# Two feed-forwards in five sets: the down products among the next set's tiles

## The chip, the cores and the metric

One core of a Trainium2 chip. The metric is the device time of one launch in microseconds. Engines: PE (TensorE, matrix products), DVE (VectorE), ACT (ScalarE), POOL (GpSimd), SP (SyncE, which issues the loads of weights). Products accumulate in PSUM, everything else lies in SBUF.

## What is computed

512 tokens of width 1024 pass two blocks in float32. The first block has two layers, each a mixer (a pooling mixer in layer 0, latent attention in layer 1) and a feed-forward, every one behind a norm and added to x:

```python
D_FF = ((8 * D_MODEL // 3 + 255) // 256) * 256
...
def swiglu(h, w_gate, w_up, w_down):
    return (jax.nn.silu(h @ w_gate) * (h @ w_up)) @ w_down
```

D_FF is 2816. The second block is a differential attention and a mixture of 16 experts with a hierarchical router. The change lies in the two feed-forwards of the first block, and by one number in the loads ahead of the experts.

## The kernel before

**Products.** x lies transposed, 8 pieces of 128 features by 512 tokens (`x[:, d]`). Every float32 operand is split into a high part rounded to fp32r and a low part, the rest; `mm3` makes three products (high x high, low x high, high x low) into one accumulator. Splitting a weight costs one ACT copy (`hi<-raw`) and one subtraction on DVE or POOL (`lo<-raw,hi`) per 512 columns.

**Stages in the trace.** Pooling mixer 0 to 36 us, feed-forward of layer 0 36 to 390, latent attention to 569, feed-forward of layer 1 569 to 927, differential attention to about 1197, routing to 1240, experts to 1519, and the end.

**One feed-forward.** `ffn` walks 22 tiles of 128 hidden features in sets, `SETS` = (0 to 8), (8 to 15), (15 to 22). A tile has gate and up weights in one load of 1 MB (`ffn_gu`, 128x2048). Its two results give silu(gate) times up, split into `hh`, `hl`. After a set's tiles, eight down products follow, one for each d of 128 output features, over the set's 7 or 8 hidden tiles (`ffn_dn`, 448 or 512 KB each), and each is added into `x[:, d]`. The rule for a tile has three forms:
- `plain(j)` for the first five: 2 x 8 x 3 products of 512 columns on `xh`, `xl`, while `mixed_x` makes sums and differences of the halves of the tokens.
- `later()` for tile 5 and for the tiles 1 and 4 of the later sets (`BETWEEN`): also 48 products of 512 columns, on the even and odd pieces (`bh`, `bl`).
- `mixed()` for the others, 12 per layer: seven products over half the rows and half the tokens each (Strassen's scheme with 7 instead of 8), 84 matmuls of 256 columns, from sums of quarters of the weights. Additions on DVE put the seven accumulators together (`t`, `u`); ACT takes the silu; then `t<-t,u`, `hh`, `hl`.

**The stream of weights.** `Stream` keeps one list of items in order of use. It has 2 raw buffers and 3 each for high and low parts (`BUFS`). `load` issues a DMA on SP as soon as a raw buffer has been handed back; in the queue it waits there for the last operation that read the buffer. `split_mixed` is the split of a mixed tile in eight steps: POOL adds r + s (`rs<-raw`) and subtracts p - r (`raw<-raw`); ACT and DVE split p, q (1024 wide), then rs; DVE makes rs - p (`raw<-rs,raw`) and q minus that (`raw<-raw`); one 512-wide split; and last q, r, s together, 1536 wide, whose `lo` hands the raw buffer back. `split_part` splits other items by 512 columns; the second part of a down load goes to POOL (`POOLED`). The calls `ws.pump()` between products do one step each; `go()` does one step of the list `tail`, which holds the end of a tile (hidden parts). Each engine works strictly in the order in which the code issues its instructions, so the places of `pump` and `go` set the order of DVE. Nearly all instructions are recorded under the helper's line, 447; the loads under 136.

**After the layers.** In the last set `after(d)` makes what the next stage needs of each finished d (`xh`, `xl`, squares summed in `ss`). `AHEAD` says how many pieces of expert weights may be loaded into free buffers before the routing is done.

Of the kernel before, what the change touches and what calls it, by code (L numbers as in the profile page):

```python
# [9 lines left out]
F32R = mybir.dt.float32r  # L10
# [3 lines left out]
OP = mybir.AluOpType  # L14
# [3 lines left out]
P = 128  # L18
# [3 lines left out]
KT = D // P  # L22
FF = 2816
FT = FF // P


SETS = ((0, 8), (8, 15), (15, 22))
PLAIN = 6
BETWEEN = (1, 4)
H = T // 2  # L30


# [7 lines left out]

AHEAD = (24, 28, 32)
PIECES = 5
CHUNKS = 7
LASTS = 2
# [44 lines left out]
class Stream:  # L91
# [473 lines left out]
class Net:  # L565
# [346 lines left out]
    def ffn(self, l, hooks, after, extra=None):  # L912
# [3 lines left out]
        nc = self.nc  # L916
        hooks = list(hooks)
        xh, xl = self.held
        parts = [[] for _ in range(7)]
        full = []  # L920
        mix = self.mixed_x(l, full, parts)
        hh, hl, pend = [], [], []

        tail = []
# [7 lines left out]
        def rest():  # L932
            while tail:
                go()

        def hidden(t):
            hh.append(self.tmp("hh", F32R))
            hl.append(self.tmp("hl", F32R))
            h, r = hh[-1], hl[-1]
            nc.scalar.activation(h, t, AF.Copy)  # L940
            yield
            nc.vector.tensor_tensor(r, t, h.bitcast(F32), op=OP.subtract)

        def evac(pg, pu):
            t, u = self.tmp("t"), self.tmp("u")
            nc.vector.tensor_tensor(t, pg, self.R, op=OP.mult)
            nc.scalar.activation(t, t, AF.Silu)
            nc.vector.tensor_tensor(u, pu, self.R, op=OP.mult)
            yield
            nc.vector.tensor_tensor(t, t, u, op=OP.mult)  # L950
            yield from hidden(t)

        def plain(j):
            wh, wl = self.ws.take()
            pp = []

            def mm(m, k, begin, end):
                o = (2 * m + k % 2) * T + k // 2 * P
                c = slice(o, o + P)
                self.mm3(pp[m], wh[:, c], wl[:, c], xh[k], xl[k], begin, end)  # L960

            if j == PLAIN - 2:
                pp += [self.acc(), self.acc()]
                for k in range(KT):
                    for m in range(2):
                        mm(m, k, k == 0, k == KT - 1)
                    xh[k] = xl[k] = None
                    if k < 2:
                        go()
                    if k > 1:  # L970
                        next(mix, None)
                    if k == 4:
                        self.ws.pump(4)
            else:
                for m in range(2):
                    pp.append(self.acc())
                    for n, k in enumerate((0, 2, 4, 6, 1, 3, 5, 7)):
                        mm(m, k, n == 0, n == KT - 1)
                        if n in (0, 2):
                            go()  # L980
                        if not hooks and n in (1, 3, 6):
                            next(mix, None)
                    self.ws.pump(3)
                    if hooks:
                        hooks.pop(0)()
            self.ws.release()
            pend.append(pp)
            if not hooks:
                while pend:
                    tail.append(evac(*pend.pop(0)))  # L990
                    go()

        def later():
            wh, wl = self.ws.take()
            pp = []
            for m in range(2):
                ps = self.acc()
                for n, k in enumerate((0, 2, 4, 6, 1, 3, 5, 7)):
                    o = (2 * m + k % 2) * T + k // 2 * P
                    c = slice(o, o + P)  # L1000
                    self.mm3(ps, wh[:, c], wl[:, c], *full[k], n == 0, n == KT - 1)
                    go()
                    self.ws.pump()
                pp.append(ps)
            self.ws.release()
            t = self.tmp("t")
            nc.scalar.activation(t, pp[0], AF.Silu)
            nc.vector.tensor_tensor(t, t, pp[1], op=OP.mult)
            tail.append(hidden(t))
            go()  # L1010

        def mixed():
            g, s = self.tmp("t"), self.tmp("u")
# [22 lines left out]
            for n in range(7):  # L1036
                if n % 2 == 0:
                    ps = self.acc()
# [13 lines left out]
                    nc.scalar.activation(g, g, AF.Silu)  # L1052
            add(s0, s0, bank[6])
            nc.vector.tensor_tensor(g, g, s, op=OP.mult)
            tail.append(hidden(g))
            go()

        for f0, f1 in SETS:
            hh.clear()
            hl.clear()  # L1060
            for j in range(f0, f1):
                if j < PLAIN - 1:
                    plain(j)
                elif j < PLAIN:
                    for _ in mix:
                        pass
                    later()
                elif self.plain(j):
                    later()
                else:  # L1070
                    mixed()
            rest()
            for d in range(KT):
                wh, wl = self.ws.take()
                ps = self.acc()
                n = f1 - f0
                for f in range(n):
                    c = slice(f * P, (f + 1) * P)
                    self.mm3(ps, wh[:, c], wl[:, c], hh[f], hl[f], f == 0, f == n - 1)
                    if f % 3 == 1:  # L1080
                        self.ws.pump()
                self.ws.flush()
                self.ws.release()
                nc.vector.tensor_tensor(self.x[:, d], ps, self.x[:, d], op=OP.add)
                if f1 == FT:
                    after(d)

    def plain(self, j):
        return j < PLAIN or any(f0 and j - f0 in BETWEEN for f0, f1 in SETS if f0 <= j < f1)

    def ffn_weights(self, l, arena=0):
        for f0, f1 in SETS:
            for j in range(f0, f1):
                self.ws.add(self.a["ffn_gu"][l, j], j < arena, not self.plain(j))
            for d in range(KT):
                self.ws.add(self.a["ffn_dn"][l, d, :, f0 * P:f1 * P])


    def rope_tables(self):
# [1286 lines left out]
def _host(inp):  # L2386

    f = np.ascontiguousarray
    o = {}
# [6 lines left out]
    def twice(v):  # L2396
# [11 lines left out]
    gu = np.stack([inp["ffn_w_gate"], inp["ffn_w_up"]], axis=0)  # L2408
    o["ffn_gu"] = f(gu.reshape(2, 2, KT // 2, 2, P, FT, P).transpose(1, 5, 4, 0, 3, 2, 6)
                    .reshape(2, FT, P, 2048))  # L2410
    o["ffn_dn"] = f(inp["ffn_w_down"].reshape(2, FT, P, KT, P).transpose(0, 3, 2, 1, 4)
                    .reshape(2, KT, P, FT * P))

    wd = inp["mla_w_down"][0]
    wd = np.concatenate([wd, wd[:, 512:]], axis=1)
# [26 lines left out]
    r = np.arange(P)  # L2442
# [4 lines left out]
    c = np.arange(T)[None, :] - 3 * P - r[:, None]  # L2447
# [58 lines left out]
```

## Time and profile before

| | us |
|---|---|
| median of 3 runs | 1537.18 (1536.66 to 1541.72) |
| the profiled execution | 1539.18 |
| its span in the trace | 1537.4 |
| PE busy | 1487.6 |
| DVE busy | 1088.1 |
| ACT busy | 815.8 |
| POOL busy | 414.0 |

The profile records one execution; the span runs from the first to the last instruction, and 1.8 us of the execution's time lie outside. Mean granted clock of PE: 0.983 of full speed. A duration in the trace is one instruction's own; where instructions overlap in an engine's pipeline, the distance of their starts is what each costs.

### The profile page before, as it was taken

To read this page: it belongs to the slowest core of one execution; us is meant where nothing else is said; L and a number is where in the kernel's file an instruction comes from. 1 tells how busy PE (TensorE), PEld (TensorE's weight loads), DVE (VectorE), ACT (ScalarE), POOL (GpSimd) and SP (SyncE) were. 2 spreads that over 40 slices of the span, in tenths; PEclk is the share of its full clock that TensorE was granted. 3 is DMA by queue.
4 is the path that set the end of the run, shared out by engine and by line. 5 is a ranking of instruction groups with operands and counts; after the bars stand their busy time and mean duration, and the time that the engine had idled before them with its cause. 6 is when DMAs were issued, how large, how long until landed. Compare 5 with 4: busy or idle time off the path is not lost.

```text
span 1537.4 us, 23426 instructions
## 1 busy us (share of the span) xinstructions
PE 1487.6 (97%) x8561; PEld 1250.4 (81%) x8561; DVE 1088.1 (71%) x1948; ACT 815.8 (53%) x1609; POOL 414.0 (27%) x330
## 2 busy tenths in 40 slices
PE   8999999999999999999999999999979799999996
PEld 7788898998878878888989989999968566666664
DVE  6795684775578747945746766888985487878774
ACT  5443343344466534423423454787774377777774
POOL 3322322222341103233222224222312222222321
PEclk9999999999999999999999999999979799999998
DMA  6124223224211112152232242122048799999991
GB/s 218 60 71 122 87 93 115 107 80 127 81 64 49 49 55 93 65 158 104 74 117 105 79 127 84 56 83 95 31 135 305 216 323 347 368 363 356 367 316 26
DMA packets 72247, 221.72 MB, mean 144 GB/s; under 512 B 7872, under 2 KB 17216, under 8 KB 58944
## 3 DMA queue, kind: packets, MB, share of 16 engines
q1 hardware_dynamic: 58752, 201.03, 37.6%
q0 software_dynamic: 4064, 14.16, 4.0%
q10 hardware_dynamic: 9312, 5.01, 1.1%
q8 instruction: 68, 1.11, 0.3%
q14 instruction: 51, 0.42, 0.1%
HBM read 208.63 MB, written 11.53 MB: 143 GB/s over the span
## 4 chain that ended last, share of the span: by engine, by line
PE 82%; DVE 7%; ACT 5%; DMA 2%; issue 1%; POOL 1%; ACTq 0%; POOLq 0%; SPq 0%; DVEq 0%
PE acc L447 70%; PE pss L447 8%; PE pst L447 4%; DVE lo L447 1%; DVE bl L447 1%; ACT hi L447 1%; ACT p L447 1%; DMA raw<-ffn_gu 1%; DVE xl L447 1%; DMA bnd<-bands 1%; DVE t L447 1%; DVE p L447 1%; DVE x L447 0%; DMA out<-ring,idx 0%; DVE xe L447 0%
## 5 line engine op out<-in xcount | busy, mean ns | idle before, releaser
L447 ACT ACTIVATE hi<-raw 128x512 fp32r<-128x512 f32 (+3 forms) x354 | 235.7, 697 | 211.2 <-PE acc L447 95.8
L447 POOL TENSOR_TENSOR lo<-raw,hi 128x512 fp32r<-128x512 f32 (+2 forms) x125 | 167.0, 1340 | 629.7 <-ACT hi L447 600.4
L447 PE MATMUL acc<-bl,hi 128*128 128x256 f32 (+1 forms) x832 | 252.5, 304 | 0.0
L447 PE MATMUL acc<-bh,hi 128*128 128x256 f32 (+1 forms) x832 | 252.5, 303 | 0.0
L447 PE MATMUL acc<-bh,lo 128*128 128x256 f32 (+1 forms) x832 | 252.4, 303 | 0.0
L447 DVE TENSOR_TENSOR lo<-raw,hi 128x512 fp32r<-128x512 f32 (+2 forms) x229 | 230.9, 1010 | 28.5 <-ACT hi L447 28.0
L447 DVE TENSOR_TENSOR wl<-raw,wh 128x512 fp32r<-128x512 f32 x288 | 203.0, 748 | 53.0 <-ACT wh L447 46.0
L447 ACT ACTIVATE wh<-raw 128x512 fp32r<-128x512 f32 x320 | 177.5, 620 | 0.0
L447 PEld LDWEIGHTS acc<-bl,hi 128*128 128x128 f32 x832 | 159.0, 191 | 6.6
L447 PEld LDWEIGHTS acc<-bh,hi 128*128 128x128 f32 x832 | 159.0, 191 | 6.6
L447 PEld LDWEIGHTS acc<-bh,lo 128*128 128x128 f32 x832 | 159.0, 191 | 6.3
L447 DVE TENSOR_TENSOR x<-acc,x 128x512 f32<-128x512 f32 x75 | 51.4, 689 | 128.7 <-PE acc L447 128.6
L447 PE MATMUL acc<-hl,hi 128*128 128x512 f32 x352 | 137.1, 390 | 0.2 <-DVE hl L447 0.2
L447 PE MATMUL acc<-hh,hi 128*128 128x512 f32 x352 | 137.1, 390 | 0.2 <-ACT hh L447 0.2
L447 PE MATMUL acc<-hh,lo 128*128 128x512 f32 x352 | 136.9, 389 | 0.0
L447 PE MATMUL acc<-hi,xh 128*128 128x256 f32 x384 | 111.6, 291 | 0.0
L447 PE MATMUL acc<-lo,xh 128*128 128x256 f32 x384 | 109.2, 284 | 0.6 <-DVE lo L447 0.6
L447 PE MATMUL acc<-hi,xl 128*128 128x256 f32 x384 | 109.0, 284 | 0.0
L447 PE MATMUL acc<-wh,teh 128*96 128x512 f32 x224 | 103.1, 460 | 0.2 <-ACT teh L447 0.2
L447 PE MATMUL acc<-wl,teh 128*96 128x512 f32 x224 | 88.2, 394 | 0.8 <-DVE wl L447 0.8
L447 PE MATMUL acc<-wh,tel 128*96 128x512 f32 x224 | 88.5, 395 | 0.0
L447 PE MATMUL acc<-xh,hi 128*128 128x512 f32 x200 | 79.8, 399 | 1.2 <-ACT xh L447 1.2
(349 smaller groups left out, 3349.9 us busy)
## 6 DMA issues: line engine op xcount, KB each, us to landing
raw<-moe_w SPq DMA_DIRECT2D x200, 256.0 KB, 8.1
raw<-moe_w SPq DMA_DIRECT2D x46, 1024.0 KB, 11.1
raw<-ffn_gu SPq DMA_DIRECT2D x43, 1024.0 KB, 4.8
raw<-ffn_dn SPq DMA_DIRECT2D x32, 448.0 KB, 3.3
raw<-da_in SPq DMA_DIRECT2D x12, 1024.0 KB, 5.0
raw<-ffn_dn SPq DMA_DIRECT2D x16, 512.0 KB, 3.5
raw<-mla_up SPq DMA_DIRECT2D x4, 832.0 KB, 4.4
raw<-mla_o_a SPq DMA_DIRECT2D x12, 256.0 KB, 3.5
```

The lines of the kernel that those rows point to most:

```text
L447: r = f(*args, **kw)
```

## The change

- `SETS` becomes five sets of 4, 4, 4, 5 and 5 tiles; `BETWEEN` goes, so all 16 tiles from the seventh on are mixed (84 matmuls of 256 columns), and only tile 5 is `later`.
- The down products of a set come among the next set's tiles. `ffn_order` gives the order of everything: after a tile, `down` for a pair of d (two accumulators, 2 x 4 or 2 x 5 hidden tiles x 3 products); after tile 5 two pairs, after tiles 6 to 15 and 17 to 20 one, after 16 and 21 none; the last set's eight d follow at the end. Down weights are repacked in pairs of d on the host (`ffn_dn0` to `ffn_dn4`, 512 or 640 KB).
- These accumulators come from the pool `pss`, those of the last set from `acc`. The addition into x goes into `tail`, so `go` issues it, a few products later.
- `hh`, `hl` come from `pair`, so that two sets' hidden parts can live at once.
- `AHEAD` for the second phase is 27 instead of 28.

```diff
-SETS = ((0, 8), (8, 15), (15, 22))
+SETS = ((0, 4), (4, 8), (8, 12), (12, 17), (17, 22))
 PLAIN = 6
-BETWEEN = (1, 4)
...
-AHEAD = (24, 28, 32)
+AHEAD = (24, 27, 32)
...
-            tail.append(hidden(t))
+            tail.append(hidden(t, hh, hl))
...
+        def down(n, i):
+
+            f0, f1 = SETS[n]
+            his, los = sets[n]
+            wh, wl = self.ws.take()
+            last = n == len(SETS) - 1
+            for m in range(2):
+                while len(tail) > 1:
+                    go()
+                ps = self.acc() if last else self.pss()
+                for f in range(f1 - f0):
+                    c = slice((m * (f1 - f0) + f) * P, (m * (f1 - f0) + f + 1) * P)
+                    self.mm3(ps, wh[:, c], wl[:, c], his[f], los[f], f == 0, f == f1 - f0 - 1)
+                    if f % 2:
+                        go()
+                        self.ws.pump()
+                d = 2 * i + m
+                if last:
+                    self.ws.flush()
+                    rest()
+                    nc.vector.tensor_tensor(self.x[:, d], ps, self.x[:, d], op=OP.add)
+                    after(d)
+                else:
+                    tail.append(add(d, ps))
+            self.ws.release()
...
+    def ffn_order(self):
+
+
+        todo = []
+        for n, (f0, f1) in enumerate(SETS):
             for j in range(f0, f1):
...
+                yield "tile", n, j
+                if j >= PLAIN - 1:
+                    for _ in range(-(-len(todo) // (f1 - j))):
+                        yield "down", n - 1, todo.pop(0)
+            todo = list(range(KT // 2))
+        for i in todo:
+            yield "down", len(SETS) - 1, i
...
     def ffn_weights(self, l, arena=0):
...
+        for kind, n, i in self.ffn_order():
+            if kind == "tile":
+                self.ws.add(self.a["ffn_gu"][l, i], i < arena, i >= PLAIN)
+            else:
+                self.ws.add(self.a[f"ffn_dn{n}"][l, i])
```

How this moves instructions shows at two places. The first is the queue of SP, which issues the loads of weights, in layer 0. Before, a set's gate-up loads follow each other, then its eight down loads:

```order
L136 DMA raw<-ffn_gu 128x2048 x8
L136 DMA raw<-ffn_dn 128x1024 x8
L136 DMA raw<-ffn_gu 128x2048 x7
L136 DMA raw<-ffn_dn 128x896 x8
L136 DMA raw<-ffn_gu 128x2048 x7
L136 DMA raw<-ffn_dn 128x896 x8
```

With the change the same queue reads so from its first gate-up load:

```order
L134 DMA raw<-ffn_gu 128x2048 x6
L134 DMA raw<-ffn_dn 128x1024 x2
L134 DMA raw<-ffn_gu 128x2048
L134 DMA raw<-ffn_dn 128x1024
L134 DMA raw<-ffn_gu 128x2048
L134 DMA raw<-ffn_dn 128x1024
L134 DMA raw<-ffn_gu 128x2048
L134 DMA raw<-ffn_dn 128x1024
L134 DMA raw<-ffn_gu 128x2048
```

It goes on in this way; the sets of five stand here:

```order
L134 DMA raw<-ffn_gu 128x2048
L134 DMA raw<-ffn_dn 128x1024
L134 DMA raw<-ffn_gu 128x2048 x2
L134 DMA raw<-ffn_dn 128x1280
L134 DMA raw<-ffn_gu 128x2048
L134 DMA raw<-ffn_dn 128x1280
L134 DMA raw<-ffn_gu 128x2048
```

Gate-up and down loads now alternate from tile 6 on, except between the tiles 16 and 17.

The second place is DVE in layer 0 in the steady part, from the split of one mixed tile's weights to the end of that split. `raw` is the loaded weights, `rs` the sum of two quarters, `t` and `u` the two results of the tile before, `acc` and `pss` accumulators. Before, with two mixed tiles behind each other or a plain one behind a mixed one (here the latter):

```order
L447 TENSOR_TENSOR lo<-raw,hi 128x1024
L447 TENSOR_TENSOR u<-t,acc 128x256
L447 TENSOR_TENSOR t<-t,acc 128x256
L447 TENSOR_TENSOR u<-u,acc 128x256
L447 TENSOR_TENSOR raw<-rs,raw 128x512
L447 TENSOR_TENSOR lo<-rs,hi 128x512
L447 TENSOR_TENSOR u<-u,acc 128x256
L447 TENSOR_TENSOR t<-t,u 128x512
L447 TENSOR_TENSOR hl<-t,hh 128x512
L447 TENSOR_TENSOR raw<-raw 128x512
L447 TENSOR_TENSOR lo<-raw,hi 128x512
L447 TENSOR_TENSOR lo<-raw,hi 128x1536
```

With the change, a mixed tile with a down pair behind it:

```order
L445 TENSOR_TENSOR u<-t,acc 128x256
L445 TENSOR_TENSOR t<-t,acc 128x256
L445 TENSOR_TENSOR u<-u,acc 128x256
L445 TENSOR_TENSOR raw<-raw 128x512
L445 TENSOR_TENSOR u<-u,acc 128x256
L445 TENSOR_TENSOR t<-t,u 128x512
L445 TENSOR_TENSOR hl<-t,hh 128x512
L445 TENSOR_TENSOR lo<-raw,hi 128x512
L445 TENSOR_TENSOR x<-pss,x 128x512
L445 TENSOR_TENSOR lo<-raw,hi 128x1536
L445 TENSOR_TENSOR x<-pss,x 128x512
L445 TENSOR_TENSOR lo<-raw,hi 128x512
```

The rows of the split stand between the previous tile's additions in both; new are two additions into x (`x<-pss,x`), one ahead of the 1536-wide `lo` and one behind it, and the `lo` of the down weights after them.

In all, PE has 8901 matmuls where it had 8613; on the operands of `later` and `mixed` (`bh`, `bl`) 32 of 512 columns remain of 160 for each kind of product, and 896 of 256 columns stand where 672 did. Additions into x number 106 where 75 were (42 from `acc`, 64 from `pss`).

## Rows read from the trace of the kernel before

**Rows 1.** The page: span; busy time of each engine (share of the span, instructions).

```profile
span 1537.4 us, 23426 instructions
...
PE 1487.6 (97%) x8561; PEld 1250.4 (81%) x8561; DVE 1088.1 (71%) x1948; ACT 815.8 (53%) x1609; POOL 414.0 (27%) x330
```

**Rows 2.** Windows: busy us of PE, PEld, DVE, ACT, POOL; PE clock granted, DMA share, GB/s.

```profile
105.00:390.00 285.00, 285.00 (x1733) 256.66 (x1732) 183.93 (x269) 110.04 (x175) 75.00 (x54) 1.00 0.31 100
...
640.00:927.20 287.20, 286.78 (x1739) 257.53 (x1737) 182.60 (x268) 115.14 (x182) 78.23 (x67) 1.00 0.32 104
...
1240.00:1519.00 279.00, 278.53 (x1288) 181.44 (x1289) 223.34 (x359) 210.87 (x417) 73.73 (x56) 1.00 0.94 324
```

**Rows 3.** Timeline of PE in layer 0: start, duration, engine, line, operation, tiles, shape, count.

```profile
168.87 0.28 PE L447 MATMUL acc<-bh,hi 128*128 128x256 f32 x1
...
178.94 0.40 PE L447 MATMUL acc<-bh,hi 128*128 128x512 f32 x1
...
189.85 0.28 PE L447 MATMUL acc<-bh,hi 128*128 128x256 f32 x1
```

**Rows 4.** Timeline of DVE in layer 0, 169 to 187 us.

```profile
169.68 1.75 DVE L447 TENSOR_TENSOR lo<-raw,hi 128x1536 fp32r<-128x1536 f32 x1
...
177.71 0.42 DVE L447 TENSOR_TENSOR u<-t,acc 128x256 f32<-128x256 f32 x1 [0.76 <-PE acc L447]
178.16 0.42 DVE L447 TENSOR_TENSOR t<-t,acc 128x256 f32<-128x256 f32 x1
178.50 0.41 DVE L447 TENSOR_TENSOR u<-u,acc 128x256 f32<-128x256 f32 x1
...
181.28 0.41 DVE L447 TENSOR_TENSOR u<-u,acc 128x256 f32<-128x256 f32 x1
181.79 0.69 DVE L447 TENSOR_TENSOR t<-t,u 128x512 f32<-128x512 f32 x1
183.19 1.00 DVE L447 TENSOR_TENSOR hl<-t,hh 128x512 fp32r<-128x512 f32 x1 [0.70 <-ACT hh L447]
184.11 1.77 DVE L447 TENSOR_TENSOR raw<-rs,raw 128x512 f32<-128x512 f32 x1
185.81 0.68 DVE L447 TENSOR_TENSOR lo<-rs,hi 128x512 fp32r<-128x512 f32 x1
186.41 0.68 DVE L447 TENSOR_TENSOR raw<-raw 128x512 f32<-128x512 f32 x1
```

**Rows 5.** Timeline of SP (DMA issues) and POOL, the same stretch.

```profile
171.46 0.33 SPq L136 DMA_DIRECT2D raw<-ffn_gu  x1
...
177.01 0.33 SPq L136 DMA_DIRECT2D raw<-ffn_gu  x1
...
181.82 1.82 POOL L447 TENSOR_TENSOR rs<-raw 128x512 f32<-128x512 f32 x1 [2.15 <-DMA raw<-ffn_gu]
183.72 1.62 POOL L447 TENSOR_TENSOR raw<-raw 128x512 f32<-128x512 f32 x1
```

**Rows 6.** DMA issues of gate and up weights, median us to landing: all; the slowest alone.

```profile
raw<-ffn_gu SPq DMA_DIRECT2D x39, 1024.0 KB, 4.8
...
raw<-ffn_gu SPq DMA_DIRECT2D x1, 1024.0 KB, 7.2
```

**Rows 7.** Groups of DVE, 640 to 927.2 us: busy, mean ns, idle before and what ended it.

```profile
L447 DVE TENSOR_TENSOR wr<-wr,vecs 128x160 f32<-128x160 f32 x1 | 0.3, 326 | 1.6 <-DMA wr<-router 1.6
```

**Rows 8.** Timeline of DVE, one of the last eight down products of layer 1.

```profile
898.84 0.69 DVE L447 TENSOR_TENSOR x<-acc,x 128x512 f32<-128x512 f32 x1 [0.93 <-PE acc L447]
900.32 0.75 DVE L447 SCALAR_TENSOR_TENSOR xl<-x,gg,xh 128x512 fp32r<-128x512 f32 x1 [0.79 <-ACT xh L447]
...
902.19 0.68 DVE L447 TENSOR_TENSOR lo<-raw,hi 128x512 fp32r<-128x512 f32 x1
```

**Rows 9.** Windows at the start of layer 1: a pause of PE and the stretch after.

```profile
573.90:576.90 3.00, 1.50 (x6) 0.51 (x4) 1.43 (x3) 2.70 (x5) 0.29 (x1) 1.00 0.69 292
576.90:583.70 6.80, 6.80 (x21) 5.74 (x21) 3.97 (x4) 2.18 (x5) 5.39 (x4) 0.50 0.35 114
```

More of the change, by code (lines that the diff above doesn't have):

```diff
@@ L934, in rest, with hidden @@
                 go()
[L936 to L939, printed above, removed]
+        def hidden(t, his, los):
+            h, r = self.pair("h")
+            his.append(h)
+            los.append(r)
             nc.scalar.activation(h, t, AF.Copy)
@@ L942, in hidden, with evac @@
             nc.vector.tensor_tensor(r, t, h.bitcast(F32), op=OP.subtract)
-        def evac(pg, pu):
+        def evac(his, los, pg, pu):
             t, u = self.tmp("t"), self.tmp("u")
@@ L950, in evac @@
             nc.vector.tensor_tensor(t, t, u, op=OP.mult)
-            yield from hidden(t)
+            yield from hidden(t, his, los)
         def plain(j):
@@ L986, in plain @@
             self.ws.release()
-            pend.append(pp)
+            pend.append([hh, hl] + pp)
             if not hooks:
@@ L1054, in mixed @@
             nc.vector.tensor_tensor(g, g, s, op=OP.mult)
-            tail.append(hidden(g))
+            tail.append(hidden(g, hh, hl))
             go()
-        for f0, f1 in SETS:
-            hh.clear()
-            hl.clear()
-            for j in range(f0, f1):
[L1062 to L1086, printed above, removed]
@@ L1088, in plain @@
-    def plain(self, j):
-        return j < PLAIN or any(f0 and j - f0 in BETWEEN for f0, f1 in SETS if f0 <= j < f1)
-    def ffn_weights(self, l, arena=0):
[L1092 to L1096, printed above, removed]
+        def down(n, i):
[22 more added lines that the diff above has]
+            self.ws.release()
@@ new lines, in add @@
+        def add(d, ps):
+            nc.vector.tensor_tensor(self.x[:, d], ps, self.x[:, d], op=OP.add)
+            return
+            yield
+        sets = {}
+        for kind, n, i in self.ffn_order():
+            if kind == "down":
+                if (n, i) == (len(SETS) - 1, 0):
+                    rest()
+                    parts = full = None
+                down(n, i)
+                if i == KT // 2 - 1:
+                    sets.pop(n)
+                continue
+            if i == SETS[n][0]:
+                hh, hl = [], []
+                sets[n] = hh, hl
+            if i < PLAIN - 1:
+                plain(i)
+            elif i < PLAIN:
+                for _ in mix:
+                    pass
+                later()
+            else:
+                mixed()
@@ new lines, in ffn_order @@
+    def ffn_order(self):
+        todo = []
+        for n, (f0, f1) in enumerate(SETS):
+            for j in range(f0, f1):
+                yield "tile", n, j
[5 more added lines that the diff above has]
+            yield "down", len(SETS) - 1, i
+    def ffn_weights(self, l, arena=0):
+        for kind, n, i in self.ffn_order():
+            if kind == "tile":
+                self.ws.add(self.a["ffn_gu"][l, i], i < arena, i >= PLAIN)
+            else:
+                self.ws.add(self.a[f"ffn_dn{n}"][l, i])
@@ L2410, in _host @@
                     .reshape(2, FT, P, 2048))
-    o["ffn_dn"] = f(inp["ffn_w_down"].reshape(2, FT, P, KT, P).transpose(0, 3, 2, 1, 4)
-                    .reshape(2, KT, P, FT * P))
+    dn = inp["ffn_w_down"].reshape(2, FT, P, KT // 2, 2, P).transpose(0, 3, 2, 4, 1, 5)
+    for n, (f0, f1) in enumerate(SETS):
+        o[f"ffn_dn{n}"] = f(dn[:, :, :, :, f0:f1].reshape(2, KT // 2, P, 2 * (f1 - f0) * P))
     wd = inp["mla_w_down"][0]
```

## The prediction

> **What bounds the kernel now.** I read the page first: TensorE (PE) is busy 97% of the span [rows 1]. Then the windows, to see whether that holds where the change lies: from 105 to 390 us, most of feed-forward layer 0, PE has no idle time at all, and from 640 to 927.2 us, layer 1, it misses 0.4 us [rows 2]. So in both feed-forwards the time is the number of PE products times their pitch, as long as the other engines keep ahead. The reader should note VectorE (DVE) in the same rows: 184 of 285 us, 65%, so it has room on the average. What the average does not tell is the order in which DVE works, and that decides here. Next the timeline of PE for the two prices: a mixed tile runs from 168.87 to 178.94, which is 10.07 us for 84 products, 0.120 each; the plain tile behind it from 178.94 to 189.85, 10.91 us for 48 products of 512 columns, 0.227 each [rows 3]. Last, the timelines of DVE, SP and POOL for how a tile's weights get ready.
>
> **Fewer PE cycles.** Four tiles per layer turn from plain to mixed, eight in all: 8 x (10.91 - 10.07) = 6.7 us less. The down products keep their number (22 x 24 per layer, 0.227 each), only their order changes. One pair of them costs 4 x 6 x 0.227 = 5.45 us with 4 tiles in the set and 5 x 6 x 0.227 = 6.81 with 5. In the steady part PE thus needs 10.07 + 5.45 = 15.52 us per cycle (a mixed tile and a pair), later 16.88.
>
> **A loop through one raw buffer.** There are two raw buffers. Before, loads of gate and up weights follow each other, so the one for the tile after next starts when the first buffer comes free, and a tile's split has a whole spare tile of PE time. In the new order of SP's queue gate-up and down loads alternate, so with two buffers every gate-up load lands in the same one: it waits for DVE's last subtraction (128x1536) of the tile just before. That subtraction stands late in DVE's order, behind the previous tile's last additions and the first addition into x. Load, split and next load form a closed loop with one tile in it, and PE is not part of it. Its length:
> - Issue to POOL's first operation: 177.01 to 181.82, 4.81 us; the median landing says 4.8 [rows 5, 6].
> - POOL's two operations, 181.82 to 183.72 + 1.62: 3.52 us [rows 5]. DVE's raw<-rs needs both; I add 0.08 as an estimate.
> - Then DVE back to back. A 512-wide operation takes a slot of 0.60 (185.81 to 186.41); the additions take 0.45 (177.71 to 178.16) and 0.34 (178.16 to 178.50); the last addition takes 0.51 (181.28 to 181.79); the product t<-t,u, with ScalarE's rounding behind it, 1.40 (181.79 to 183.19) [rows 4]. In the new order: raw<-rs 0.60, lo<-rs 0.60, u 0.45, t 0.34, u 0.34, raw<-raw 0.60, u 0.51, t<-t,u 1.40, hl 0.60, lo 0.60, x<-pss 0.60, lo of 1536 1.75 [rows 4]. Sum 8.39.
> - The next issue comes 0.03 behind: 169.68 + 1.75 = 171.43, issue at 171.46 [rows 4, 5].
>
> Together 4.81 + 3.52 + 0.08 + 8.39 + 0.03 = 16.83 us. That is 1.31 more than PE's 15.52 in a cycle with a set of 4, and 0.05 less than 16.88 with 5. The addition x<-pss is new: no row has it. Its nearest row is an operation of the same width, 0.60; it might be hidden in a wait (0) or take 1.17 more when POOL runs beside it, as raw<-rs did (1.77 from 184.11, against a slot of 0.60) [rows 4]; I take 0.60.
>
> **How long the lead lasts.** PE needs the third split part of a tile at its third product, 24 x 0.120 = 2.9 us after the tile's start and that part's lo is followed by x (0.60) and the 1536-wide lo (1.75), so the latter ends about 2.3 us later. So PE stalls where that subtraction ends later than 5.2 us after its tile starts. Tile 6 is got ready beside plain tiles, its subtraction ends about when the tile starts: a lead of 5.2. Every cycle takes 1.31 of it, and in layer 0 operations of the rope tables in DVE's order take about 0.6 more in most of them. By tile 9 the lead is gone (3 x 1.9 = 5.7, a stall of 0.5). Tiles 10 to 16 pay 1.31 each, 9.2, and three rope operations at 0.6 are in the loop with them, 1.8. Layer 0: 11.5 us. Between tiles 16 and 17 there is no down pair, so the load for 17 starts early and the cycles with 5 stay just even. In layer 1 the rope work is gone, but the router's multiply stands in DVE's order within tile 7's cycle and waits for its own load, 1.6 us now [rows 7]; I put its harm at 3 (estimate: that wait and what stands behind it), so tile 8 pays 0.5 and tiles 9 to 16 pay 8 x 1.31 = 10.5: 11.0 us. Both: 22.5 us.
>
> **The ends of the layers.** The last set's eight products are 15 x 0.227 = 3.4 us each, before 4.8. In layer 1 DVE takes 898.84 to 902.19 + 0.68, 4.03 us, per product for x, xl, the two square sums and a split [rows 8]. It falls behind by 0.62 each; the eighth xl comes at about 3.5 + 7 x 4.03 + 2.2 = 33.9 us, while PE wants it after 27.2 + 42 x 0.120 = 32.3. I take 1.9 with the square sum (0.5 if some splits move away, 3 if all stay). In layer 0 the chain has one square sum less and about keeps up: 0.5. Together 2.4.
>
> **The rest.** The first set of layer 1 lost about 1 us to a late down load; that load now comes in another place, I take 0.5 less (0 to 1). One routing piece less ahead: in the expert stage PE misses 0.5 of 279 us while DMA is 94% busy [rows 2], one 0.73 us slot at most; 0. The planner reorders part of the attention stage: 0, between -3 and +3.
>
> **Sum** against the profiled execution (1539.2 us, 1.8 outside its span; 2.0 above the median of the runs): 1539.2 - 6.7 + 22.5 + 2.4 - 0.5 = 1556.9, which is 1555 on the footing of the median.
>
> **Rivals.**
> - *The loop does not close.* If one cycle stays under PE's 15.52, which needs 1.3 us less than I count, there is no stall: -6.7 + 2.4 - 0.5 gives 1532, and 1530 if the ends cost little. For it: DVE has room on the average [rows 2], and 1.40 of my sum is a wait that other work could fill. Against: DVE works in the written order, and I counted slots, no waits of PE. The point of decision is 15.52.
> - *Half a loop.* The load lands quicker, or the lead is longer than 5.2 because the first cycles run free; the stalls are then 5 to 15 us: 1537 to 1548.
> - *The clock falls.* At the start of layer 1 PE paused (1.50 us busy of 3.00), and in the next 6.8 us the granted clock was 0.50, the lower level: 21 products where 30 fit at the full one [rows 9]. If the stall in each tile did the same, PE alone would need more than the loop: (30 - 21) x 0.227 = 2 us per cycle, less the 1.3 that it idles, over some 16 cycles 11 to 30 us: 1566 to 1585. Against: the stalls of 1.3 us are shorter, and PE is busy otherwise. The Trainium skill (TensorE: Matmul & The Clock Gate, section HAM oscillation — how this bites in real kernels) describes just this, a wait in every weight tile after which each tile begins at half clock; no repeated pause of this kind is in the trace of before. By it, the time would be the one just given.
> - *POOL gets ahead.* POOL's split of the down weights is ready some 0.6 us after DVE's 1536-wide subtraction begins. If it starts first, the subtraction is stretched as raw<-rs was, by 1.17 [rows 4], and the loop is 18.0: 16 x 1.2 + 8 x 1.1 more, 1583. The Trainium skill (SBUF — State Buffer, section Who interferes with whom) calls the port between the two an exclusive lock, with whoever issues first blocking the other; the stretched row agrees.
> - *The change does not do what it says.* The new program has 32 of the 512-wide products on each of the plain tile's operand pairs where it had 160, so the tiles are mixed indeed; I give this no chance.
>
> **Numbers.** The loop binds: 0.62, with its own range 1550 to 1566 (a load that lands 0.4 later because a down load is issued some 2 us behind it, where the slowest took 7.2 [rows 6], costs 16 x 0.4 and some for the sets of 5: +9). Half a loop: 0.18. It does not close: 0.14. Clock or POOL: 0.06. A difference of 0.3%, 4.6 us, is about what a measurement of this kernel can tell from none. Faster by more: the third case and a little of the second, 0.15; within: 0.10, out of the second; slower: 0.75. The range goes from 1532, which takes in about half of the third case, to 1566.
>
> **What would show it.** In the changed profile: PE pauses of about 1.3 us in tiles 9 or 10 to 16 of each layer, ended by DVE's lo; gate-up loads issued right behind the 1536-wide lo, about 16.8 us apart; no pauses in the cycles of 5; each feed-forward 7 to 9 us longer than before, stalls and savings together; the wait for xl or ss at the end of layer 1. Wrong would be gate-up loads issued less than 15.5 us apart with PE still full, or pauses ended by something else.

## The result and the profile after

The changed kernel took 1575.11 us (median of 4), the kernel before beside it 1536.92: a ratio of 1.0242, with a 95% interval of 1.0222 to 1.0261. It is slower, as forecast, but by 38 us where 18 had been forecast; the range ended at 1566.

The page of the changed kernel, against [rows 1] (in the third row: a group of products, its busy time and mean, and behind the second bar the idle time of PE ahead of it and what ended most of it):

```profile
span 1574.8 us, 24096 instructions
...
PE 1495.6 (95%) x8849; PEld 1267.6 (80%) x8849; DVE 1136.4 (72%) x2074; ACT 830.4 (53%) x1617; POOL 435.2 (28%) x323
...
L445 PE MATMUL acc<-bh,lo 128*128 128x256 f32 (+1 forms) x928 | 270.9, 292 | 21.9 <-DVE lo L445 21.9
```

The time of products rose by 8 us only, although the change takes matmul time away; 21.9 us of the rest are PE's waits for DVE's lo in the mixed tiles. Where the 38 us lie is read from windows cut at the first product of each stage (feed-forward 0, latent attention, feed-forward 1, the differential attention up to its last output product, the rest; columns as in [rows 2]):

```profile
36.50:402.80 366.30, 354.02 (x2179) 319.28 (x2179) 270.00 (x413) 150.89 (x236) 113.73 (x72) 0.99 0.26 92
402.80:583.30 180.50, 174.81 (x971) 146.67 (x970) 119.74 (x237) 95.48 (x216) 39.12 (x31) 1.00 0.15 49
583.30:955.70 372.40, 358.67 (x2177) 323.02 (x2176) 265.08 (x405) 151.58 (x236) 111.39 (x80) 0.98 0.29 103
955.70:1242.80 287.10, 268.27 (x1924) 251.87 (x1923) 213.87 (x552) 184.95 (x445) 72.86 (x57) 0.95 0.31 103
1242.80:1574.80 332.00, 310.40 (x1453) 200.76 (x1451) 246.29 (x431) 227.66 (x450) 85.19 (x71) 0.97 0.90 310
```

The same cuts in the trace of before give 353.3, 179.9, 357.8, 276.1 and 334.1 us; the attention's end lies at 1242.60, 0.2 us ahead of the cut above, so that the stage takes 286.9. So feed-forward 0 takes 13.0 more, feed-forward 1 14.6, the differential attention with its output products 10.8, latent attention 0.6, routing and experts 1.9 less. The forecast had 7 to 9 for each feed-forward and 0 for the attention.

**The loop is there, and about as long as worked out.** Gate-up loads, and the chain between two of them, in layer 0 (SP, POOL, DVE):

```profile
185.91 0.33 SPq L134 DMA_DIRECT2D raw<-ffn_gu  x1
...
203.11 0.33 SPq L134 DMA_DIRECT2D raw<-ffn_gu  x1
...
221.80 0.33 SPq L134 DMA_DIRECT2D raw<-ffn_gu  x1
...
238.58 0.33 SPq L134 DMA_DIRECT2D raw<-ffn_gu  x1
...
255.42 0.33 SPq L134 DMA_DIRECT2D raw<-ffn_gu  x1
```

```profile
226.59 1.30 POOL L445 TENSOR_TENSOR rs<-raw 128x512 f32<-128x512 f32 x1 [3.68 <-DMA raw<-ffn_gu]
227.97 2.15 POOL L445 TENSOR_TENSOR raw<-raw 128x512 f32<-128x512 f32 x1
```

```profile
230.15 0.69 DVE L445 TENSOR_TENSOR raw<-rs,raw 128x512 f32<-128x512 f32 x1 [1.18 <-POOL raw L445]
...
233.60 0.69 DVE L445 TENSOR_TENSOR t<-t,u 128x512 f32<-128x512 f32 x1
235.00 0.69 DVE L445 TENSOR_TENSOR hl<-t,hh 128x512 fp32r<-128x512 f32 x1 [0.70 <-ACT hh L445]
235.60 0.68 DVE L445 TENSOR_TENSOR lo<-raw,hi 128x512 fp32r<-128x512 f32 x1
236.21 0.68 DVE L445 TENSOR_TENSOR x<-pss,x 128x512 f32<-128x512 f32 x1
236.81 1.75 DVE L445 TENSOR_TENSOR lo<-raw,hi 128x1536 fp32r<-128x1536 f32 x1
```

The 1536-wide lo ends at 236.81 + 1.75 = 238.56, the next load goes out at 238.58: this turn is 16.78 us, the forecast said 16.83. It is the shortest one. The next is 16.84 long, the last of layer 0 17.02, and those ahead of tile 12, with the rope operations in them, 17.2 to 17.7 (17.20 from 185.91 to 203.11), about the 0.6 more that the forecast had given them; the turns of layer 1 without a late load and behind the router's multiply are 16.8 to 17.2. The steps shown have their forecast slots: 1.40 from the product to hl, 0.60 for the first x<-pss. PE waits in the middle of the tiles (in all, times, longest; first layer 0):

```profile
PE acc L445 <- DVE lo L445: 10.4, 6, 2.7
```

and the same in layer 1:

```profile
PE acc L445 <- DVE lo L445: 11.5, 8, 2.4
```

Against the 10.07 us of a mixed tile, by the starts of PE's products, tiles 9 to 15 of layer 0 lost 0.3, 2.0, 1.7, 4.4, 0, 1.3 and 1.5 us and tiles 16 and 17 together 5.1: 16.1. Tiles 8 to 15 of layer 1 lost 1.2, 1.4, 4.1, 0, 1.2, 1.7, 1.3, 1.7, and 16 and 17 together 6.2: 18.6. Forecast were 11.5 and 11.0. The losses of 1.2 to 2.0 are the loop: each is the turn, 16.8 to 17.5 us, less PE's 15.52. (Tile 8 of layer 1 has another late load behind its 1.2: 6.5 us beside POOL's stores of zeros, 0.47 MB, most of it paid from the lead.) The large losses have two other causes.

**A late load, and the clock.** Ahead of tile 12 the load took 6.0 us instead of 4.8:

```profile
q8 instruction: 1, 0.02, 1.5%
...
raw<-ffn_gu SPq DMA_DIRECT2D x1, 1024.0 KB, 6.0
```

A packet of the instruction queue (16 KB: the page has 1.15 MB in 70 of them) ran in the middle of it; in layer 1 the same pair (6.1 us, one such packet) stands ahead of tile 10, and in run 7 below, with the same feed-forward code, both stand there again (5.7 and 6.2). The loads of 4.8 in this trace had no such packet beside them, or only in their first 0.8 us. In all kept traces, gate-up loads in the middle of which such a packet began (0.3 to 3.2 us behind the issue, twelve cases, two of them in the trace of before) took 5.1 to 6.3 us, and 106 without one 4.6 to 5.2; loads with another gate-up load or POOL's stores beside them are left aside. That the packet is the cause is a reading of this; no run takes it away. Before, a load of 7.2 [rows 6] cost nothing, because a tile lay between. Now the pause grew to 2.9 us by the starts of the products (2.7 of idle time), and behind it the granted clock fell to the lower level, 1.2 of 2.4 GHz, for a part of the stretch:

```profile
213.40:216.50 3.10, 3.10 (x26) 2.96 (x25) 3.07 (x8) 1.15 (x2) 0.00 (x0) 1.00 0.00 0
216.50:219.50 3.00, 0.36 (x2) 0.15 (x2) 2.20 (x5) 1.95 (x3) 0.00 (x0) 0.92 0.00 0
219.50:226.40 6.90, 6.84 (x46) 6.84 (x47) 5.12 (x8) 1.88 (x5) 2.24 (x1) 0.79 0.51 181
841.20:847.60 6.40, 6.40 (x32) 6.40 (x33) 6.37 (x10) 2.32 (x4) 0.00 (x0) 0.54 0.32 105
```

The third row: 46 products in 6.9 us at a mean of 0.79, where 57 fit at 0.120; tile 12 lost 4.4 us, 2.9 in the pause and about 1.6 behind it. The last row is the stretch behind layer 1's pause in tile 16, 0.54. The shorter pauses of this trace, 1.1 to 1.9 us by the starts, have no such drop behind them. The Trainium skill (TensorE: Matmul & The Clock Gate, section HAM oscillation — how this bites in real kernels) describes waits with a slow start after each; in this trace it holds for the four longest pauses alone.

The length of a pause does not settle it, as other traces show. In run 7 the two pauses in tile 16 are as long as here (2.4 us of idle time) and the stretches behind them stay at the upper level:

```profile
289.60:296.00 6.40, 6.39 (x53) 6.39 (x54) 6.37 (x10) 2.38 (x5) 0.00 (x0) 1.00 0.30 102
835.80:842.20 6.40, 6.31 (x52) 6.31 (x53) 6.37 (x11) 2.46 (x5) 0.00 (x0) 1.00 0.31 104
```

In run 3 two pauses of 1.3 us of idle time differ; behind one the clock fell, behind the other not:

```profile
202.40:206.00 3.60, 3.58 (x17) 3.58 (x18) 3.57 (x7) 0.40 (x1) 0.00 (x0) 0.53 0.69 241
215.50:219.00 3.50, 3.45 (x28) 3.45 (x29) 3.46 (x7) 0.01 (x1) 0.00 (x0) 1.00 0.67 250
```

So what the clock took here, 1.6 to 2.8 us behind each of four pauses, is what it took in this execution; what decides it stays open.

**Tile 16.** In it PE paused two times by the starts, 0.8 us for hi and 2.5 us for lo of the third part, where the other tiles have 1.1 to 1.9 for lo alone:

```profile
280.86 1.29 POOL L445 TENSOR_TENSOR rs<-raw 128x512 f32<-128x512 f32 x1
282.23 1.62 POOL L445 TENSOR_TENSOR raw<-raw 128x512 f32<-128x512 f32 x1
```

```profile
280.93 1.77 DVE L445 TENSOR_TENSOR raw<-rs,raw 128x512 f32<-128x512 f32 x1 [1.19 <-POOL raw L445]
282.62 1.78 DVE L445 TENSOR_TENSOR lo<-rs,hi 128x512 fp32r<-128x512 f32 x1
```

No down pair lies between tiles 16 and 17, so the load for 17 lands early, as I had said, and POOL starts on it at 280.86, 0.07 us ahead of the first of DVE's two subtractions with rs in tile 16's split; POOL's second operation begins 0.39 ahead of the other. The two took 1.77 and 1.78 instead of 0.69. It is the stretched row of [rows 4], two times, inside the loop.

**The attention stage.** Some of PE's waits in it, changed kernel, 955 to 1250 us:

```profile
PE acc L445 <- DVE ol L445: 4.9, 1, 4.9
PE acc L445 <- DVE x L445: 3.5, 3, 1.3
...
PE acc L445 <- ACT oh L445: 1.7, 1, 1.7
```

Before, 926 to 1250 us and 927.2 to 1203.3:

```profile
PE acc L447 <- DVE x L447: 2.0, 3, 1.3
...
927.20:1203.30 276.10, 264.18 (x1924) 249.50 (x1923) 220.07 (x551) 183.52 (x444) 73.03 (x57) 0.96 0.35 118
```

Of the three only x stands in the trace of before (both times with 1.3 us that lie behind the stage's end); waits for l and kh that it had are gone. In all, PE is idle 19 us of the stage where it was 12, and its products take 4 us more, at a mean clock of 0.95 for 0.96.

### The profile page after: what moved, and what is told of

It is laid out like the page before. It is cut to its first block, busy times and chain, and to the rows that moved or that the text cites. A ratio compares the mean times of both kernels' runs of the same rounds, so it can differ in the third digit from the quotient of the medians.

```text
span 1574.8 us, 24096 instructions
## 1 busy us (share of the span) xinstructions
PE 1495.6 (95%) x8849; PEld 1267.6 (80%) x8849; DVE 1136.4 (72%) x2074; ACT 830.4 (53%) x1617; POOL 435.2 (28%) x323
## 3 DMA queue, kind: packets, MB, share of 16 engines
q8 instruction: 70, 1.15, 0.3%
## 5 line engine op out<-in xcount | busy, mean ns | idle before, releaser
L445 ACT ACTIVATE hi<-raw 128x512 fp32r<-128x512 f32 (+2 forms) x346 | 241.2, 727 | 188.6 <-DMA raw<-ffn_gu 88.0
L445 POOL TENSOR_TENSOR lo<-raw,hi 128x512 fp32r<-128x512 f32 (+1 forms) x102 | 156.6, 1537 | 587.8 <-ACT hi L445 551.5
L445 DVE TENSOR_TENSOR lo<-raw,hi 128x512 fp32r<-128x512 f32 (+3 forms) x244 | 247.8, 1017 | 72.4 <-ACT hi L445 72.1
L445 PE MATMUL acc<-bh,lo 128*128 128x256 f32 (+1 forms) x928 | 270.9, 292 | 21.9 <-DVE lo L445 21.9
L445 PEld LDWEIGHTS acc<-bh,lo 128*128 128x128 f32 x928 | 181.3, 195 | 26.2 <-DVE lo L445 24.9
L445 PEld LDWEIGHTS acc<-bh,hi 128*128 128x128 f32 x928 | 181.2, 195 | 4.3 <-ACT hi L445 1.8
L445 PEld LDWEIGHTS acc<-bl,hi 128*128 128x128 f32 x928 | 181.0, 195 | 2.4
L445 PE MATMUL pss<-hh,hi 128*128 128x512 f32 x272 | 106.2, 390 | 0.0
L445 PE MATMUL pss<-hl,hi 128*128 128x512 f32 x272 | 106.2, 390 | 0.0
L445 PE MATMUL pss<-hh,lo 128*128 128x512 f32 x272 | 105.8, 389 | 0.0
L445 ACT ACTIVATE t<-t 128x512 f32<-128x512 f32 x42 | 26.6, 632 | 129.1 <-DVE t L445 129.1
```

The source lines that it names most:

```text
L445: r = f(*args, **kw)
```

## The experiments

All in one table, stages in us from the traces. The ratio is that against the kernel before measured beside each run, whose medians are 1536.92 to 1541.17:

| kernel | median | ratio (95%) | layer 0 | layer 1 | attention |
|---|---|---|---|---|---|
| before | 1536.92 | | 353.3 | 357.8 | 276.1 |
| the change | 1575.11 | 1.0242 (1.0222 to 1.0261) | 366.3 | 372.4 | 286.9 |
| 1 split first | 1556.22 | 1.0123 (1.0095 to 1.0151) | 356.6 | 355.2 | 288.7 |
| 2 four plain tiles | 1552.58 | 1.0088 (1.0062 to 1.0114) | 353.5 | 355.3 | 290.2 |
| 3 all mixed only | 1580.10 | 1.0266 (1.0239 to 1.0294) | 375.6 | 374.1 | 276.9 |
| 4 a piece less | 1536.64 | 0.9984 (0.9970 to 0.9999) | 353.6 | 354.8 | 274.8 |
| 5 split first, second form | 1546.10 | 1.0055 (1.0038 to 1.0072) | 352.9 | 353.2 | 288.5 |
| 6 the same, planner's lags | 1549.71 | 1.0070 (1.0044 to 1.0096) | 352.8 | 353.6 | 290.7 |
| 7 the change, planner's lags | 1577.70 | 1.0245 (1.0207 to 1.0284) | 365.0 | 365.8 | 290.8 |
| 8 downs one tile later | 1574.56 | 1.0228, a single run | 369.1 | 366.0 | 287.4 |
| 9 as 5, fewer split steps | 1545.66 | 1.0026 (1.0010 to 1.0041) | 356.1 | 356.9 | 278.8 |
| 10 the change, fewer steps | 1571.53 | 1.0200 (1.0162 to 1.0238) | 370.3 | 372.2 | 278.0 |
| 11 half way | 1586.52 | 1.0297 (1.0273 to 1.0321) | 371.7 | 373.6 | 289.5 |
| 12 both cures | 1543.01 | 1.0019 (1.0004 to 1.0034) | 353.8 | 353.6 | 282.6 |

Layer 1 by itself moves some 3 us between executions of the same code (357.8 and 354.8 in the rows "before" and 4), and in the change 6.6 (372.4, and 365.8 in run 7, where the clock did not fall at the layer's start or behind tile 16's pause).

**1, split first.** One more step of the split after each of a mixed tile's last three products:

```diff
                 go()
-                self.ws.pump()
+                self.ws.pump(1 + (n > 3))
```

> The changed kernel with one more step of the split after each of a mixed tile's last three products, so that DVE makes the 1536-wide lo ahead of the previous tile's last addition, its product, its hidden part and the first addition into x. No work is added or taken away. Theory A (the loop through one raw buffer is too long): the loop loses 0.51 + 1.40 + 0.60 + 0.60 = 3.1 us, 16.8 - 3.1 = 13.7, under PE's 15.52; the pauses of PE at the third product (16 us in layer 0, 19 in layer 1, slow clock behind them included) go but for 0 to 4 us, and the time falls from 1575 to about 1541 to 1545. Rival B (DVE has simply too much work in these cycles, or the loads are too slow): the same work in another order changes under 5 us, 1570 to 1578. Rival C (the end of the loop only moves: the 1536-wide part now waits for the buffer that the previous tile gives back at its end): half of it, 1555 to 1562. In all of them the attention stage behind keeps its 287 us.

The pauses on lo are gone in both layers. The loads of layer 1 go out 15.4 to 15.6 us apart from tile 9 on, at PE's pace; those of layer 0 15.5 to 16.2, still a little over 15.52, so that a loop of 13.7, as worked out, is not seen there; as I read it the lead pays the rest. What PE still waits for in layer 0:

```profile
PE acc L445 <- ACT hh L445: 2.1, 1, 2.1
PE acc L445 <- DVE u L445: 1.1, 1, 1.1
```

Feed-forwards 356.6 and 355.2. Theory A stands: the same work in another order, and 27 of the 28 us that both feed-forwards had lost came back. The total of 1556 lies 11 above my figure; most of that is a new wait for hh at the last set's start in each layer (2.1 and 1.7, in layer 0 with slow products behind it), made by the extra steps, and the attention stage, slower by 2 than in the change.

**2, four plain tiles.**

```diff
+WHOLES = (9, 12, 16, 19)
...
+            elif i in WHOLES:
+                later()
...
-                self.ws.add(self.a["ffn_gu"][l, i], i < arena, i >= PLAIN)
+                self.ws.add(self.a["ffn_gu"][l, i], i < arena, i >= PLAIN and i not in WHOLES)
```

> The changed kernel, but tiles 9, 12, 16 and 19 of each layer stay plain, the same tiles as before the change: only the five sets and the interleaved down products remain of it. PE has 8 x 0.84 = 6.7 us more to do. Theory A: a plain tile's raw buffer comes free as soon as its four parts are split, so the loop is broken there and the lead of some 5 us is given back at tiles 9, 12 and 16; pauses remain in about half of the cycles of layer 0 and 1: 35 us of pauses become 5 to 15, the time is 1575 + 6.7 - 20 to 30 = 1552 to 1562. Rival B (too much DVE work): a plain tile has some 4 us less for DVE, pauses go in the same way but only in the cycles of the plain tiles, 8 x 1.3 = 10 less: about 1571.

1552.6, within the range, but partly by luck: one pause on lo is left in the two layers together (1.3 us, layer 1), where 5 to 15 us had been expected, and the attention stage grew by 3 over the change. So five sets with interleaved down products cost the feed-forwards nothing as long as plain tiles break the loop; what it takes above the kernel before lies in the attention stage, 14 us longer.

**3, all mixed only.** `BETWEEN = ()` in the kernel before.

> The kernel before, with all 16 later tiles mixed and nothing else changed. PE has 6.7 us less to do. Theory A speaks of the alternation of loads, which is not there (two gate-up loads use both buffers): no loop binds, a gain of up to 6.7 us, but without plain tiles or down products between them DVE's own slots per mixed tile (about 10 to 11 us with what POOL holds it up) meet PE's 10.07, so that some of it is lost again: 1530 to 1537. If DVE's load were the cause in the changed kernel too (rival B), the loss would be larger here than there, where DVE has 15.5 us per tile: over 1545.

A miss: 1580, where theory A had 1530 to 1537 and rival B over 1545. Seven mixed tiles in a row took 85 us (the stretch, then two of DVE's waits in it):

```profile
171.40:256.40 85.00, 76.01 (x589) 73.96 (x588) 72.02 (x106) 33.30 (x49) 15.58 (x11) 0.96 0.23 77
...
DVE lo L447 <- ACT hi L447: 5.9, 7, 1.8
DVE hl L447 <- ACT hh L447: 4.2, 6, 0.7
```

DVE is busy 72.0 of 85.0 us by durations and waits 10.1 for ACT's hi and hh: work and waits that its order puts between them come to some 12 us for a mixed tile, and PE offers 10.07. How much of it is work and how much the order was not taken apart. Here DVE's time per tile binds, as rival B says, but that does not carry to the changed kernel, where PE offers 15.52 and run 1 took the pauses away with DVE's work unchanged. It says what the plain tiles and the interleaved down products are for.

**4, a piece less.** `AHEAD = (24, 27, 32)` in the kernel before.

> The kernel before with 27 instead of 28 pieces ahead of the routing. The prediction's price: 0. Expected 1537, within 2 us, the attention stage 276 us as before, since the order of PE in it is the same. Rival: the 10 us that the attention stage lost in the changed kernel come from this number: 1545 to 1548.

No loss; that edit is not the cause of the attention's 10.8 us.

**5, split first, second form.** The extra step only where a mixed tile is next to be split:

```diff
                 self.ws.pump()
+                if n > 3 and self.ws.split in self.ws.mixed:
+                    self.ws.pump()
```

> As the kernel with the split first, but the added steps are made only where the next item to split is a mixed tile, so that the layer's last tile no longer lets its hidden part wait behind the split of the last down weights. Theory A: the pause of 2.1 (1.7) us on hh at the start of the last set's products goes, with the slow clock behind it; layer 0 takes 350 to 352 us (before the change 353.3, with it 366.3), layer 1 351 to 354 (357.8, 372.4), the attention stage stays at 287 to 290: 1543 to 1548 in all. Rival: the pause comes from something else and stays, 1554 to 1558.

As expected, but for 0.9 us in layer 0: the wait for hh is gone, 352.9 and 353.2. The change's 3.4 us per layer are not all there: 2.5 us in layer 0 and 1.1 in layer 1 still go at tiles 16 and 17.

**6 and 7, the planner's lags.**

```diff
+        plan = self.nc
+        now = plan.free["pe"]
+        for k, v in (("act", 2.55), ("dve", 3.5), ("pool", 0.84)):
+            plan.free[k] = now + v
+        for t in plan.there, plan.read:
+            for k in t:
+                t[k] = min(t[k], now + 3.65)
```

> The same, and the planner of the attention stage starts from the lags that it had before the change (ACT 2.55, DVE 3.5, POOL 0.84 us behind PE instead of 6.6, 7.55, 5.46; nothing in flight ready later than 3.65), which changes only the order in which that stage's instructions are written. Theory D (the 10 us that the attention stage lost are the planner's: it believes that DVE is late after the shorter last products, and writes an order that is 6 us longer by its own reckoning): the stage takes 276 to 282 us, the total 1530 to 1537, under the kernel before. Rival E (the stage is slower for another reason, the loads of its weights or DVE really being late): it stays at 286 to 290, total as in the run beside it.

> The changed kernel with nothing but the planner's state at the attention stage put back as in the run before this. Theory D: the stage takes 276 to 282 us instead of 287, the total 1564 to 1570. Rival E: 1573 to 1577.

Theory D falls: 290.7 and 290.8, longer than with the lags as they were. In these traces PE's products in the stage stand in a third order, the same in both and neither that of before nor that of the change.

**8, downs one tile later.** In `ffn_order`, for the sets of five, `len(todo) // (f1 - j)` in place of the rounded-up quotient.

> The changed kernel with the down pairs of the sets of five moved by one tile: none behind tiles 12 and 17, one behind each of 13 to 16 and 18 to 21. Two gate-up loads then follow each other at tiles 12 to 13 and 17 to 18 instead of 16 to 17. Theory F (the long pause at tile 16, 0.8 + 2.5 us, comes from the next tile's load: it lands early, POOL starts on it, and DVE's two subtractions with rs take 1.77 beside POOL instead of 0.69): the long pause moves to tile 12, 2.5 to 3.5 us with a stretched raw<-rs there, and another one comes at tile 17; tile 16 pauses 1.3 as the others or not at all. Rival G (tile 16 pauses for something of its own, the change of the set's size): it stays at tile 16.

The pair of pauses (2.1 and 2.9 us by the starts) is now in tile 12 of layer 0, with the same two stretched rows:

```profile
213.15 1.75 DVE L445 TENSOR_TENSOR raw<-rs,raw 128x512 f32<-128x512 f32 x1 [1.19 <-POOL raw L445]
214.82 1.78 DVE L445 TENSOR_TENSOR lo<-rs,hi 128x512 fp32r<-128x512 f32 x1
```

In layer 0 tiles 12 and 17 lose 7.8 and 6.3 us with their neighbours, tile 16 0.3. Layer 1 has the stretched rows in tiles 12 and 17 too, but tile 16 also loses 4.0 there, behind a load of 6.3. Theory F stands.

**9 and 10, fewer split steps.** In `down`:

```diff
-                        self.ws.pump()
+                        if not (last and i > 1):
+                            self.ws.pump()
```

> The kernel with the split first (second form), and in the last two pairs of the last set no split steps between the products: the attention stage then begins with fewer of its own weights split ahead. The planner then writes PE's order of that stage as before the change. Theory H (the 10 us come from the order that the planner writes when more split weights are at hand, and neither from its lags nor from the chip): the attention stage takes 275 to 279 us instead of 287 to 290; with 353 and 353 us for the feed-forwards the time is 1530 to 1536, under the kernel before by 3 to 8 us. Rival I (DVE is really late at that point after the shorter products): 286 to 290, total 1544 to 1549.

> The changed kernel with nothing but those split steps left out in the last two pairs of each layer. Theory H: the attention stage takes 275 to 279 us, the feed-forwards stay at 366 and 366 to 372 (one or two us more if the first weights of the next stage come late): 1562 to 1568. Rival I: 1573 to 1579.

The attention stage takes 278.8 and 278.0: theory H stands. The order of PE's products in it is that of before again, product for product. Over all fourteen traces order and time go together: the order of before in runs 3, 4, 9, 10 and 12 (274.8 to 282.6, with 276.1 before), that of the change in the change itself and in runs 1, 2, 5, 8 and 11 (286.9 to 290.2). A run that puts back the order alone, with the steps as in the change, is not among them. The price is at the seams: PE now waits for the first weights of each next stage, in run 10

```profile
PE acc L445 <- ACT hi L445: 3.8, 1, 3.8
```

and 2.6 us behind layer 0. That is most of why the totals miss my figures, by 10 us in run 9 and by 4 in run 10.

**11, half way.** As 5, but with `n == 6` in place of `n > 3`.

> The changed kernel with one more split step after a mixed tile's last product alone: DVE then makes the third split part ahead of the previous tile's last addition, and the 1536-wide lo ahead of the first addition into x; all else stands as in the change. Theory A in numbers: the loop is 0.60 shorter, 16.2 us, 0.7 over PE's 15.52 instead of 1.3, and the pauses come at the fifth product (the 1536-wide part) instead of the third; they start two tiles later and are half as long, so of 35 us of pauses and slow clock 14 to 20 remain, 1555 to 1562 in all with the attention stage as in the change. Rival J (not the loop but the late third part alone causes the pauses): they go altogether, 1541 to 1547.

A miss, and an instructive one: 1587, most loads 17.2 to 17.8 us apart. The pauses did move to the fifth product, but the loop became longer, not shorter:

```profile
254.23 0.63 ACT L445 ACTIVATE hh<-t 128x512 fp32r<-128x512 f32 x1 [1.82 <-DVE t L445]
254.77 2.51 ACT L445 ACTIVATE hi<-raw 128x1536 fp32r<-128x1536 f32 x3
```

```profile
252.44 0.69 DVE L445 TENSOR_TENSOR lo<-raw,hi 128x512 fp32r<-128x512 f32 x1 [0.28 <-ACT hi L445]
...
254.89 0.69 DVE L445 TENSOR_TENSOR hl<-t,hh 128x512 fp32r<-128x512 f32 x1 [0.70 <-ACT hh L445]
256.27 1.76 DVE L445 TENSOR_TENSOR lo<-raw,hi 128x1536 fp32r<-128x1536 f32 x1 [0.68 <-ACT hi L445]
```

DVE waits 0.28 and 0.68 us for ACT's hi; the 1536-wide one stands behind hh in ACT's order. The DVE slot that I had taken out of the loop was a cover for ACT's two roundings. The loss again equals the excess: a turn of 17.3 less 15.5 is 1.8, and the tiles with such turns lost 1.7 to 2.0. In all the tiles lost 17.8 and 19.3 us, little more than in the change (16.1 and 18.6); the rest of what run 11 takes beyond it is mostly a wait for hh at the last set's start, as in run 1 (3.9 and 3.8 with the slow products behind it), and the attention stage.

**12, both cures.** As 5, and in layer 1 alone five split steps fewer in the last two pairs.

> The split first (second form), and five split steps fewer in the last two pairs of layer 1 alone, so that layer 0's end keeps its cover and PE's order in the attention stage is that of before the change. Layer 0 353 us, layer 1 353 to 355, attention stage 276 to 279: 1532 to 1538, against 1537 to 1541 of the kernel before beside it. If leaving out the steps costs the start of the attention stage as much as it did with eight steps less (some 3 us, the first xl and weights late): 1537 to 1541, no difference.

1543.0 against 1539.3: within 0.3% of the kernel before, not faster. The start of the attention stage pays 2.9 us for a late hi, and tiles 16 and 17 lose 3.5 and 2.9 (in run 5 2.5 and 1.1), so that it lies above both ranges expected. No version with the five sets is faster than the kernel before.

## Why the prediction was wrong

**Right: the sign, its place and its mechanism.** The loop through one raw buffer, 16.83 forecast and 16.8 to 17.2 measured where no late load, rope operation or router's multiply stood in it, with pauses at the third product, ended by DVE's lo, in the tiles from 10 (8 in layer 1) to 16 but for the one behind each late load; no loss in the cycles with sets of five; run 1 removes it by order alone, and run 11 lengthens it and the loss grows a little. The saving of eight plain tiles was there: mixed tiles without a pause take 10.07. The first addition x<-pss took its 0.60.

**Wrong: the attention stage.** "The planner reorders part of the attention stage: 0, between -3 and +3" measured +10.8. The step that failed is the price of nothing for what the planner would write. Run 10 shows where it comes from: not the piece less (run 4), nor the planner's lags alone (runs 6, 7), but how many of that stage's weights are split when the planning begins. The paired down weights of the last set have fewer parts than the eight single ones had, the same number of steps goes on into the next stage's weights, and the planner writes another order, in which the output products wait for oh and ol. Why that order is slower was not taken apart further. These are 10.8 of the 20 us by which the forecast missed.

**Wrong: the size of the stalls**, 34.7 us for 22.5, 12 more. Two terms:
- "The load for 17 starts early and the cycles with 5 stay just even": the cycles did; the early load itself hurt tile 16. I had the lock between POOL and DVE as a rival for the down weights' split, and priced the pair of gate-up loads at nothing. About 3.7 us in layer 0, 4.9 in layer 1, slow products included; in run 7, without them, tiles 16 and 17 lost 3.5 and 3.4 in place of 5.1 and 6.2.
- The load's price: a median of 4.8 in a loop without slack. I held the slowest load of before only in the range. The turns with loads of 6.0 and 6.1 us cost 4.4 and 4.1 where 1.3 was counted: the load's 1.2 and, behind the longer pause, a lower clock. After each the loop had gained on PE, so that the next tile lost nothing; that gave 1.3 back each.

**The end of layer 1**, forecast at 1.9 us, cost under 1 (waits of 0.2 on xl and on ss, and a few products that came slower). DVE did fall behind, as counted:

```profile
943.18 0.68 DVE L445 TENSOR_TENSOR x<-acc,x 128x512 f32<-128x512 f32 x1
...
947.13 0.68 DVE L445 TENSOR_TENSOR x<-acc,x 128x512 f32<-128x512 f32 x1
```

From there to the eighth product it takes 3.95 us for each where PE takes 3.40, 0.55 more; 0.62 had been counted. The eighth xl was ready 32.7 us after the last set's start, not 33.9, and PE waited 0.2 us for it.

The clock rival had a share where I gave it none in the sum: 1.6 to 2.8 us behind each of the four longest pauses in this execution. "It does not close" and "half a loop" are ruled out.

## What to carry to other kernels

When two kinds of loads alternate through two buffers, each kind has one buffer; write down the closed loop from a load's issue over every instruction that stands in front of the one that frees the buffer, on each engine, and compare it with what the bounding engine needs per turn. A loop above that price is paid in every turn once the lead is gone, each late load is then paid in full, and a shorter chain on one engine may only uncover another's. When a planner writes a later stage from the state it finds, a change in how far the stream of weights has got can cost nearly as much as the stage that was changed (10.8 us here, against 13.0 and 14.6): look at the order of the stages behind it before pricing them at nothing.

## What was not expected of the hardware

A load of 1 MB took 5.1 to 6.3 us instead of 4.8 where a packet of the instruction queue of 16 KB began 0.3 to 3.2 us behind its issue (twelve cases in all kept traces). Two of DVE's 512-wide subtractions took 1.77 us instead of 0.69 where POOL had begun 0.07 and 0.39 us earlier, and run 8 moved both together. And equal pauses of PE did not have equal ends: of those of 2.5 to 2.9 us by the starts, all four in the changed kernel were followed by 3.4 to 6.9 us at a mean of 0.54 to 0.79, but two of the four in run 7 by none; pauses of 1.1 to 1.9 left the clock at its upper level in the changed kernel, and some of 1.5 in run 3 did not.
